# A kernel of attention and convolution on one core: edge rows wrapped in two steps, output weights prepared during attention

## The chip, the core and the metric

One core of a Trainium2 chip runs the kernel. The metric is the device time of one execution in microseconds. TensorE multiplies matrices, VectorE (DVE) and ScalarE (ACT) work on what it leaves in PSUM, GpSimd (POOL) works on SBUF, and SyncE (SP) issues nearly all transfers, in order, from one queue. The same 16 DMA engines carry all of them.

## The reference, cut to what matters

`_layer` is applied to a sample of 4096 rows (called s) and to a prompt of 1024 rows (p), both 1024 wide, in float32:

```python
proj = x @ w_in                                  # q, k, v, gate | three 512-wide inputs u_h | gate
attn = weights * three dilated windows of attention over q, k, v   # weights: softmax of their lse
u = _short_conv(u_h, conv_w, conv_b)             # out[t] = b + u[t-1] w0 + u[t] w1 + u[t+1] w2, zero beyond the ends
z = u[..., :C]
for n in range(2):
    z = u[..., (n + 1) * C:(n + 2) * C] * (_two_sided_fftconv(z, filters...) + hyena_d[n] * z)
mixed = concat(_rms(attn, attn_norm_g) * silu(g_attn), _rms(z, hyena_norm_g) * silu(g_hyena))
out = mixed @ w_out
y = layernorm(alpha * x + out)
```

## The kernel before

Products run in two rounded parts: an operand is split into a high part (`rnd`, usually ScalarE) and a remainder (`rest`, VectorE or POOL), and three products are summed.

Two chains of generators are woven together by `_interleave`, which gives each step a nominal length and always takes the chain that is behind; a step may yield the name of a flag and is held until that flag is in `self.done`. A planner then orders each engine's instructions by this order and by simulated readiness, so that what is emitted early has precedence. The first chain is `proj_first` (u0, u1, v; rows in groups of 128, first s, then p), `proj_second` (u2, k, q), `attention` (which begins with the gate), `last` and `output`. The second is `filters`, `convs`, `hyena`. Attention needs the PSUM that `convs` holds; `hyena` runs beside attention, its last eight row groups (those of p) after it, and `output` follows them.

A group r of 128 rows holds the positions a * R + r, so the neighbour of a row lies in the next or the previous group at the same a, and `short_conv` adds whole groups. Only group 0 and group R - 1 need a neighbour that is shifted by one a. Their parts go to a DRAM tile `e` (four parts of 128 rows), and a function `wrap` (lines 438 to 444) finishes them: it zeroes a tile on VectorE, loads 127 shifted rows of `e` into it, loads the other part, adds the two on POOL (line 417) and stores a row group of `u`, all at one place of the program. There are 12 wraps (three inputs, two sequences, two ends). Those of u0 and u1 of s run in the first group of p, those of p at the end of the first step of `proj_second`, those of u2 of s after its last group there, and those of u2 of p late in the gate of attention. `conv_in` reads u0 from group 0 on, after the flag `u_s`.

`conv_in`, `conv_mid` and `conv_out` are the convolution by two-stage Fourier transforms, with intermediate results in DRAM (X, B, G).

`output` loads w_out in 16 pieces of 128 x 512 by `load_w` (lines 382 to 395): load, scale by the norm weights `ng` (line 392), `rnd` to `wo h`, `rest` to `wo l` (line 227). Its loop multiplies the three attention results (`oo`, line 1271), normalizes, transposes and projects.

Of the kernel before, what the change touches and what calls it, by code (L numbers as in the profile page):

```python
# [10 lines left out]
F32 = mybir.dt.float32  # L11
# [186 lines left out]
class _Kernel:  # L198
# [31 lines left out]
    def scratch(self, ctx):  # L230
        dp = self.pool(ctx, "dram", 1, DRAM)
        self.S = {}
        for nm, L in SEQS:
            NB = L // N1
            self.S[nm] = dict(
                L=L, NB=NB, A=L // 16,
                x=self.I["x_" + nm],
                R=L // P,
                u=[dp.tile([L, C], F32, name=f"u{i}_" + nm) for i in range(3)],
                e=[dp.tile([4, P, C], F32, name=f"e{i}_" + nm) for i in range(3)],  # L240
                qT=dp.tile([C, L], F32, name="qT_" + nm),
                kT=dp.tile([C, L], F32, name="kT_" + nm),
                v=dp.tile([L, H, VW], BF16, name="v_" + nm),
                o=dp.tile([3, L, H, 66], F32, name="o_" + nm),
                G=[dp.tile([2 * N1, NB, C], F32, name=f"G{i}_" + nm) for i in range(2)],
                X=[dp.tile([2 * N1, NB, C], F32, name=f"X{i}_" + nm) for i in range(2)],
                B=[dp.tile([2 * NB, N1, C], F32, name=f"B{i}_" + nm) for i in range(2)],
                xT=dp.tile([D, L], F32, name="xT_" + nm),
                ga=dp.tile([L, C], F32, name="ga_" + nm),
                mx=dp.tile([L, C], F32, name="mx_" + nm),  # L250
            )

    def globals_(self, ctx):
        nc = self.nc
        gp = self.pool(ctx, "one")
        self.ident = gp.tile([P, P], F32, name="ident")
        with self.tc.high_priority():
            nc.sync.dma_start(out=self.ident, in_=self.I["ident"])
        self.one = gp.tile([P, 1], F32, name="one")
        nc.vector.memset(self.one, 1.0)  # L260

# [153 lines left out]
    def short_conv(self, tp, w, st, nm, i, r, ps, later):  # L415
# [3 lines left out]
        R, e = S["R"], S["e"][i]  # L419
# [18 lines left out]
        def wrap(tp, src, dst, part, row, tags=("m2", "m2")):  # L438
            z, y = (tp.tile([P, C], F32, name=tag) for tag in tags)
            nc.vector.memset(z, 0.0)  # L440
            nc.sync.dma_start(out=z[dst], in_=e[src][slice(1, P) if dst.start == 0 else slice(0, P - 1)])
            nc.sync.dma_start(out=y, in_=e[part])
            add(y, z)
            nc.sync.dma_start(out=ur[row], in_=y)

        later.append(lambda tp, **k: wrap(tp, 0, slice(0, P - 1), 3, R - 1, **k))
        later.append(lambda tp, **k: wrap(tp, 2, slice(1, P), 1, 0, **k))


    def proj_first(self, ctx):  # L450
# [49 lines left out]
        for b, (nm, r) in enumerate(work):  # L500
            S = self.S[nm]
            for ci in range(3):
# [22 lines left out]
                if r == 0 and later:  # L525
                    for f in later:
                        f(tp)
                    self.done.add("u_" + work[b - 1][0])
                    later.clear()
                yield 5.3  # L530
            cur, nxt = nxt, []
        self.later = later


    def proj_second(self, ctx):
# [37 lines left out]
        for b, (nm, g) in enumerate(work):  # L573
# [39 lines left out]
            if b == 0:  # L613
                for f in self.later:
                    f(tp)
                self.done.add("u_" + SEQS[-1][0])
            if last and b < len(work) - 1:
                for f in later:
                    f(tp)
                later.clear()  # L620
            self.later = later
# [9 lines left out]
    def convs(self, ctx):  # L631
# [3 lines left out]
        yield "u_" + a  # L635
        yield from self.conv_in(a)
        yield from self.conv_mid(a, 0)
        yield "u_" + b
# [5 lines left out]
        yield from self.conv_mid(b, 1)  # L644
        yield "qk"
# [19 lines left out]
    def conv_in(self, nm):  # L665
        nc, S = self.nc, self.S[nm]
        zr = S["u"][0].rearrange("(m n) c -> n m c", n=S["NB"])
        for n2 in range(0, S["NB"], 2):
            z = self.slot("z", ZB)
            for j in range(2):  # L670
                nc.sync.dma_start(out=z[64 * j:64 * j + 64], in_=zr[n2 + j])
            self.conv_dft(nm, 0, n2, z)
            yield 2.0

    def conv_mid(self, nm, n):
# [7 lines left out]
        for s in range(NB):  # L683
            x = self.slot("x", XB)
# [82 lines left out]
    def attention(self, ctx):  # L767
# [79 lines left out]
        with ExitStack() as gx:  # L847
            for i, v in enumerate(self.gate(gx)):
# [5 lines left out]
                if i >= 9 * BOOT and i % 10 == 0 and self.later:  # L854
                    self.later.pop(0)(lp, tags=("kT", "qT"))
# [288 lines left out]
    def hyena(self, ctx):  # L1144
# [4 lines left out]
        with self.tc.high_priority():  # L1149
            (wh, wl), = self.load_w(wp, self.stage(tp, "x", (NK, P), 2), self.I["w_in"][0], [7 * C], "wg")  # L1150
        yield "att"
        for nm, L in SEQS:
# [6 lines left out]
            for r in range(R):  # L1159
                x = tp.tile([P, NK, P], F32, name="x")  # L1160
# [46 lines left out]
    def output(self, ctx):  # L1207
# [6 lines left out]
        stp = [lambda: tp.tile([P, D], F32, name="hh", bufs=hbufs)[:, 0:512]]  # L1214
        ng = wp.tile([P, NK], F32, name="ng")
        nc.sync.dma_start(out=ng[:, 0:4], in_=self.I["attn_norm_g"][0].rearrange("(k p) -> p k", p=P))
        nc.sync.dma_start(out=ng[:, 4:8], in_=self.I["hyena_norm_g"][0].rearrange("(k p) -> p k", p=P))
        wt = {i: [wp.tile([P, NK, 512], F32R, name=f"wo{k}{i}") for k in "hl"] for i in range(2)}
# [13 lines left out]
        with self.tc.high_priority():  # L1232
            nxt = load(*work[0])
            wo = self.load_w(wp, stp, self.I["w_out"][0], [0, C], "wo", scale=ng, tiles=wt)
# [159 lines left out]
```

## Time and profile before

| | us |
|---|---|
| median of 3 runs | 4419.52 |
| lowest and highest | 4416.1, 4421.64 |
| the profiled execution | 4421.58 |
| its span in the profile | 4419.8 |

| engine | busy us of the span |
|---|---|
| TensorE (PE) | 4038.2 (91%) |
| VectorE (DVE) | 3218.0 (73%) |
| ScalarE (ACT) | 2152.8 (49%) |
| GpSimd (POOL) | 2003.6 (45%) |

How to read the rows: a row of the windows has the stretch in us from the start of the span, its length, the busy time and the number of instructions of PE, of its weight loads (PEld), of DVE, ACT and POOL, then the granted TensorE clock as a share of 2.4 GHz, the mean busy share of the 16 DMA engines and the GB/s that they moved. A row of the chain of waits has a start, a duration and what lasted so long; SPq is the queue that issues transfers, and a DMA row is a transfer from its issue to its landing. A row of the waits names who waited for whom, the total, the count and the longest. A row of the groups has line, engine, operation, output and input, shapes, count, then total and mean ns. A row of the timeline has a start, a duration, engine, line and operation.

### The profile page before, as it was taken

Reading aid. Unit: us, or ns where it says so; the run is one execution under the profiler, and the core shown is the slowest. Engines: PE = TensorE matmul, PEld = TensorE weight load, DVE = VectorE, ACT = ScalarE, POOL = GpSimd, SP = SyncE. Lnnn points to the kernel's source line nnn. Section 1 sums busy time; section 2 is a strip of 40 time slices with the busy share of each in tenths; the row PEclk is TensorE's granted clock in tenths of the full one; section 3 lists DMA queues with packets and bytes.
Section 4 is the critical chain, followed back from the end, with each engine's and each line's share of the span. In section 5 each row is a group of like instructions: output and inputs, shape, how many; then the busy total and the mean of one; then the engine's idle time right before and its main releaser. Section 6 shows DMA issues by size and latency. Waiting matters only on the chain.

```text
span 4419.8 us, 87947 instructions
## 1 busy us (share of the span) xinstructions
PE 4038.2 (91%) x31996; PEld 3416.6 (77%) x31996; DVE 3218.0 (73%) x6503; ACT 2152.8 (49%) x4246; POOL 2003.6 (45%) x1714
## 2 busy tenths in 40 slices
PE   7999999868789999998989979999999999689897
PEld 6999999858579876887867647888888887477776
DVE  7889888447678754575788666878787877677774
ACT  3433334245344444443465446777777776223332
POOL 4444444335567731366655251414141432266664
PEclk9999999979899999999989988999999999799999
DMA  5555555579555579754566665656565556644441
GB/s 182 180 179 171 178 171 176 178 223 284 166 162 165 165 253 285 230 160 142 170 211 195 215 205 152 175 154 170 155 180 153 153 159 176 217 169 173 173 173 67
DMA packets 662475, 800.87 MB, mean 181 GB/s; under 512 B 68024, under 2 KB 400014, under 8 KB 662042
## 3 DMA queue, kind: packets, MB, share of 16 engines
q1 hardware_dynamic: 643610, 762.64, 55.4%
q0 software_dynamic: 18432, 32.60, 3.2%
q8 instruction: 254, 4.16, 0.4%
q14 instruction: 179, 1.47, 0.1%
HBM read 499.22 MB, written 295.80 MB: 180 GB/s over the span
## 4 chain that ended last, share of the span: by engine, by line
PE 55%; DMA 13%; DVE 10%; POOL 7%; issue 6%; ACT 3%; SPq 2%; POOLq 0%; DVEq 0%; ACTq 0%
PE qk L401 10%; PE u L401 10%; PE pv L950 6%; PE sc L891 5%; PE pt L924 4%; PE g L1182 4%; PE g L1131 3%; POOL hh L1309 2%; DMA oo<-o_s 2%; POOL oo L1271 2%; PE pf L215 2%; PE g L215 2%; PE pz L215 2%; PE c L735 1%; PE c L215 1%
## 5 line engine op out<-in xcount | busy, mean ns | idle before, releaser
L223 POOL TENSOR_SCALAR qc<-q 128x256 fp32r<-128x256 f32 x352 | 246.9, 719 | 707.6 <-PE sc L891 702.0
L401 PE MATMUL u<-wuh,xh 128*128 128x256 f32 x1920 | 556.2, 290 | 10.0 <-ACT wuh L219 9.2
L401 PE MATMUL u<-wul,xh 128*128 128x256 f32 x1920 | 549.1, 286 | 2.2 <-DVE wul L227 2.0
L401 PE MATMUL u<-wuh,xl 128*128 128x256 f32 x1920 | 547.7, 285 | 2.1 <-DVE xl L227 2.1
L227 DVE TENSOR_TENSOR x<-x,xh 128x512 fp32r<-128x512 f32 x320 | 357.7, 1140 | 248.4 <-ACT xh L219 245.6
L915 ACT ACTIVATE sb<-sb,ob 128x192 f32<-128x192 f32 (+2 forms) x960 | 412.2, 473 | 39.9 <-DVE ob L906 31.3
L401 PEld LDWEIGHTS u<-wuh,xh 128*128 128x128 f32 x1920 | 371.6, 194 | 22.8 <-ACT wuh L219 10.4
L401 PEld LDWEIGHTS u<-wul,xh 128*128 128x128 f32 x1920 | 371.8, 194 | 11.9 <-DVE wul L227 3.0
L401 PEld LDWEIGHTS u<-wuh,xl 128*128 128x128 f32 x1920 | 371.4, 193 | 9.9 <-DVE xl L227 2.9
L401 PE MATMUL qk<-xh,wql 128*128 128x256 f32 x1280 | 364.2, 285 | 0.7 <-DVE wql L227 0.5
L401 PE MATMUL qk<-xh,wqh 128*128 128x256 f32 x1280 | 364.4, 285 | 0.0
L401 PE MATMUL qk<-x,wqh 128*128 128x256 f32 x1280 | 364.2, 285 | 0.0
L927 ACT ACTIVATE th<-pt 96x512 f16<-96x512 f32 (+2 forms) x480 | 272.1, 576 | 177.7 <-PE pt L924 174.8
L950 PE MATMUL pv<-V,th 128*128 128x64 bf16 (+3 forms) x5568 | 334.8, 194 | 0.0
L950 PE MATMUL pv<-V,tl 128*128 128x64 bf16 (+3 forms) x3712 | 324.5, 195 | 8.5 <-DVE tl L935 5.4
L935 DVE TENSOR_TENSOR tl<-pt,th 96x512 f16<-96x512 f32 (+2 forms) x480 | 316.2, 667 | 18.8 <-ACT th L927 16.6
L704 POOL TENSOR_TENSOR z<-fa,fi 128x512 f32<-128x512 f32 x160 | 246.2, 1539 | 151.2 <-DVE fi L703 150.5
L227 POOL TENSOR_TENSOR g<-g,gh 128x512 fp32r<-128x512 f32 x160 | 221.1, 1383 | 183.0 <-ACT gh L219 171.4
L219 ACT ACTIVATE xh<-x 128x512 fp32r<-128x512 f32 x400 | 241.9, 633 | 127.4 <-DMA x<-xT_s 42.2
L950 PEld LDWEIGHTS <-th 128*128 128x128 f16 (+1 forms) x5568 | 291.5, 98 | 2.2 <-issue 2.2
L950 PEld LDWEIGHTS <-tl 128*128 128x128 f16 (+1 forms) x3712 | 252.1, 98 | 51.1 <-DVE tl L935 17.6
L924 PE MATMUL pt<-ident,sb 128*128 128x128 f32 (+1 forms) x1856 | 291.1, 283 | 0.3 <-DVE tl L935 0.3
(223 smaller groups left out, 12021.5 us busy)
## 6 DMA issues: line engine op xcount, KB each, us to landing
G_s<-go SPq DMA_DIRECT2D x128, 256.0 KB
g<-G_s SPq DMA_DIRECT2D x128, 256.0 KB
x<-X_s SPq DMA_DIRECT2D x128, 256.0 KB
B_s<-bo SPq DMA_DIRECT2D x128, 256.0 KB
x<-xT_s SPq DMA_DIRECT2D x64, 512.0 KB
oo<-o_s SPq DMA_DIRECT2D x32, 792.0 KB
u_s<-m SPq DMA_DIRECT2D x96, 256.0 KB
V<-v_s SPq DMA_DIRECT2D x168, 145.5 KB
```

Source lines behind the costliest of these rows:

```text
L215: nc.tensor.matmul(out=out, lhsT=l, rhs=r, start=(i == 0), stop=(i == n - 1))
L219: self.nc.scalar.activation(out, in_, AF.Copy, scale=scale)
L223: self.nc.gpsimd.tensor_scalar(out=out, in0=in_, scalar1=scale, scalar2=0.0, op0=ALU.mult, op1=ALU.add)
L227: e.tensor_tensor(out=out, in0=in_, in1=hi.bitcast(F32), op=ALU.subtract)
L401: nc.tensor.matmul(out=out, lhsT=l, rhs=r, start=(k == 0 and i == 0), stop=(k == len(pairs) - 1 and i == len(ops) - 1))
L704: nc.gpsimd.tensor_tensor(out=z, in0=fa, in1=fi, op=ALU.add)
L891: nc.tensor.matmul(out=st["sc"][i], lhsT=qv[half, x], rhs=f(y)[half], start=(j == 0), stop=(j == 2))
L915: nc.scalar.activation(sb[:, i, 0:W], sb[:, i, 0:W], AF.Exp, bias=st["ob"][:, ui, i, 65:66], scale=-1.0)
L924: nc.tensor.transpose(out=pt[0:n, i, t], in_=st["pr"][:, i, t * n:(t + 1) * n], identity=self.ident)
L927: nc.scalar.activation(th[0:n, :, 0:nkt], pt[0:n, :, 0:nkt], AF.Copy)
L935: e.tensor_tensor(out=tl[0:n, :, 0:nkt], in0=pt[0:n, :, 0:nkt], in1=th[0:n, :, 0:nkt], op=ALU.subtract)
L950: last = nc.tensor.matmul(out=pv[:, 0:w], lhsT=st[p][0:n, i, t], rhs=vv[:, VC[b]:VC[b] + w], start=(t == 0 and j == 0), stop=(t == nkt - 1 ...
```

## The change

`e` gets a row of zeros at either end of its groups, stored once at the start, so that a shifted load reads 128 rows. `wrap` becomes two steps, `begin` (allocate and load) and `end` (add and store); `wrap_step` runs the `end` of the wraps begun before and begins one more. Steps are made in the row groups of p in `proj_first`, in `conv_mid`, and in the gate of attention. `conv_in` takes its row pairs from the middle on, each behind a flag of its row group, and the four that touch wrapped groups last, behind the flag `w_s` or `w_p`. `hyena` prepares the output's weights: in its row groups from the third on, one piece each, loaded, scaled, split and stored in a DRAM tile `wo`, in the buffer that its own input `x` uses. `output` only loads `wo`, in eight transfers of 1 MB.

```diff
--- before.py
+++ after.py
@@ -229,6 +229,7 @@
...
         dp = self.pool(ctx, "dram", 1, DRAM)
+        self.wo = dp.tile([2, NK, P, 2, 512], F32, name="wo")
         self.S = {}
@@ -237,7 +238,7 @@
...
                 u=[dp.tile([L, C], F32, name=f"u{i}_" + nm) for i in range(3)],
-                e=[dp.tile([4, P, C], F32, name=f"e{i}_" + nm) for i in range(3)],
+                e=[dp.tile([4, P + 2, C], F32, name=f"e{i}_" + nm) for i in range(3)],
                 qT=dp.tile([C, L], F32, name="qT_" + nm),
@@ -258,6 +259,13 @@
...
         nc.vector.memset(self.one, 1.0)
+        zero = gp.tile([P, C // P], F32, name="zero")
+        nc.vector.memset(zero, 0.0)
+        for nm, _ in SEQS:
+            for e in self.S[nm]["e"]:
+                for k, row in ((0, P + 1), (2, 0)):
+                    nc.sync.dma_start(out=e[k, row].rearrange("(p f) -> p f", p=P), in_=zero)
+        self.wraps, self.adds = [], []
@@ -416,7 +424,7 @@
...
         mul = lambda o, x: nc.vector.tensor_tensor(out=o, in0=ps, in1=x, op=ALU.mult)
-        R, e = S["R"], S["e"][i]
+        R, e = S["R"], [S["e"][i][k, 1:P + 1] for k in range(4)]
         ur = S["u"][i].rearrange("(a r) c -> r a c", r=R)
@@ -435,16 +443,27 @@
...
-        def wrap(tp, src, dst, part, row, tags=("m2", "m2")):
-            z, y = (tp.tile([P, C], F32, name=tag) for tag in tags)
-            nc.vector.memset(z, 0.0)
-            nc.sync.dma_start(out=z[dst], in_=e[src][slice(1, P) if dst.start == 0 else slice(0, P - 1)])
-            nc.sync.dma_start(out=y, in_=e[part])
-            add(y, z)
-            nc.sync.dma_start(out=ur[row], in_=y)
-
-        later.append(lambda tp, **k: wrap(tp, 0, slice(0, P - 1), 3, R - 1, **k))
-        later.append(lambda tp, **k: wrap(tp, 2, slice(1, P), 1, 0, **k))
+        def wrap(src, part, row):
+            def begin(tp, tags, **kw):
+                z, y = (tp.tile([P, C], F32, name=tag, **kw) for tag in tags)
+                nc.sync.dma_start(out=z, in_=src)
+                nc.sync.dma_start(out=y, in_=e[part])
+
+                def end():
+                    add(y, z)
+                    nc.sync.dma_start(out=ur[row], in_=y)
+                return end
+            return begin
+
+        later.append(wrap(S["e"][i][0, 2:P + 2], 3, R - 1))
+        later.append(wrap(S["e"][i][2, 0:P], 1, 0))
+
+    def wrap_step(self, *args, **kw):
+        for f in self.adds:
+            f()
+        self.adds = [f(*args, **kw) for f in self.wraps[:1]]
+        self.wraps = self.wraps[1:]
+        return not self.adds
@@ -522,14 +541,13 @@
...
                                   in_=vt.rearrange("p h c -> p (h c)"))
-                if r == 0 and later:
-                    for f in later:
-                        f(tp)
-                    self.done.add("u_" + work[b - 1][0])
-                    later.clear()
+                if nm != SEQS[0][0] and "w_" + SEQS[0][0] not in self.done and self.wrap_step(tp, ("wz", "wy"), bufs=1):
+                    self.done.add("w_" + SEQS[0][0])
+                if r == S["R"] - 1:
+                    self.wraps, later = later, []
+                self.done.add(f"u_{nm}{r}")
                 yield 5.3
             cur, nxt = nxt, []
-        self.later = later
@@ -610,15 +628,8 @@
...
                 yield 5.3
-            if b == 0:
-                for f in self.later:
-                    f(tp)
-                self.done.add("u_" + SEQS[-1][0])
-            if last and b < len(work) - 1:
-                for f in later:
-                    f(tp)
-                later.clear()
-            self.later = later
+            if last:
+                self.wraps, later = later, []
             cur, nxt = nxt, []
@@ -632,16 +643,17 @@
...
         a, b = (nm for nm, _ in SEQS)
-        yield "u_" + a
         yield from self.conv_in(a)
         yield from self.conv_mid(a, 0)
-        yield "u_" + b
         yield from self.conv_in(b)
...
         yield from self.conv_mid(b, 1)
+        for f in self.adds:
+            f()
+        self.adds = []
         yield "qk"
@@ -665,7 +677,12 @@
...
         zr = S["u"][0].rearrange("(m n) c -> n m c", n=S["NB"])
-        for n2 in range(0, S["NB"], 2):
+        R, NB = S["R"], S["NB"]
+        steps = [(f"u_{nm}{r + 2}", n2) for r in range(2, R - 2, 2) for n2 in (r, r + R)]
+        steps += [("w_" + nm, n2) for n2 in (R - 2, NB - 2, 0, R)]
+        for flag, n2 in steps:
+            if flag not in self.done:
+                yield flag
             z = self.slot("z", ZB)
@@ -681,6 +698,8 @@
...
         for s in range(NB):
+            if self.wrap_step(self.ct, ("fa", "fi"), bufs=2) and f"u_{SEQS[-1][0]}{self.S[SEQS[-1][0]]['R'] - 1}" in self.done:
+                self.done.add("w_" + SEQS[-1][0])
             x = self.slot("x", XB)
@@ -851,8 +870,8 @@
...
                     self.lead = None
-                if i >= 9 * BOOT and i % 10 == 0 and self.later:
-                    self.later.pop(0)(lp, tags=("kT", "qT"))
+                if i >= 9 * BOOT and i % 10 == 0:
+                    self.wrap_step(lp, ("kT", "qT"))
                 yield v
@@ -1148,6 +1167,21 @@
...
             (wh, wl), = self.load_w(wp, self.stage(tp, "x", (NK, P), 2), self.I["w_in"][0], [7 * C], "wg")
+        ng = wp.tile([P, NK], F32, name="ng")
+        nc.sync.dma_start(out=ng[:, 0:4], in_=self.I["attn_norm_g"][0].rearrange("(k p) -> p k", p=P))
+        nc.sync.dma_start(out=ng[:, 4:8], in_=self.I["hyena_norm_g"][0].rearrange("(k p) -> p k", p=P))
+        chunks = [(i, k) for i in range(2) for k in range(NK)]
+
+        def out_weights():
+            i, k = chunks.pop(0)
+            t = tp.tile([P, NK, P], F32, name="x").rearrange("p (a b) n -> p a (b n)", a=2)
+            lo, hi = t.bitcast(F32R)[:, 0], t.bitcast(F32R)[:, 1]
+            nc.sync.dma_start(out=t[:, 0], in_=self.I["w_out"][0, k * P:(k + 1) * P, i * 512:i * 512 + 512])
+            nc.vector.tensor_scalar_mul(t[:, 0], t[:, 0], ng[:, k:k + 1])
+            self.rnd(hi, t[:, 0])
+            self.rest(lo, t[:, 0], hi)
+            nc.sync.dma_start(out=self.wo[i, k], in_=t)
+
         yield "att"
@@ -1157,6 +1191,8 @@
...
             for r in range(R):
+                if chunks and r > 1:
+                    out_weights()
                 x = tp.tile([P, NK, P], F32, name="x")
@@ -1211,11 +1247,7 @@
...
         hbufs = 2 * G
-        stp = [lambda: tp.tile([P, D], F32, name="hh", bufs=hbufs)[:, 0:512]]
-        ng = wp.tile([P, NK], F32, name="ng")
-        nc.sync.dma_start(out=ng[:, 0:4], in_=self.I["attn_norm_g"][0].rearrange("(k p) -> p k", p=P))
-        nc.sync.dma_start(out=ng[:, 4:8], in_=self.I["hyena_norm_g"][0].rearrange("(k p) -> p k", p=P))
-        wt = {i: [wp.tile([P, NK, 512], F32R, name=f"wo{k}{i}") for k in "hl"] for i in range(2)}
+        wt = {i: [wp.tile([P, NK, 512], F32, name=f"wo{k}{i}") for k in "lh"] for i in range(2)}
         work = [(nm, n2) for nm, L in SEQS for n2 in range(0, L // P, G)]
@@ -1231,7 +1263,11 @@
...
             nxt = load(*work[0])
-            wo = self.load_w(wp, stp, self.I["w_out"][0], [0, C], "wo", scale=ng, tiles=wt)
+            for i in range(2):
+                for k in range(0, NK, 4):
+                    for t, w in enumerate(wt[i]):
+                        nc.sync.dma_start(out=w[:, k:k + 4], in_=self.wo[i, k:k + 4, :, t].rearrange("k p n -> p k n"))
+            wo = [[t.bitcast(F32R) for t in wt[i][::-1]] for i in range(2)]
         lng = wp.tile([P, D], F32, name="lng")
...
         nc.sync.dma_start(out=lng, in_=self.I["ln_g"][0:1].to_broadcast([P, D]))
```

## Rows read from the trace of the kernel before

**Rows 1.** Windows of the kernel before, stage by stage.

```profile
860.00:1085.00 225.00, 167.39 (x1191) 157.43 (x1190) 117.22 (x148) 95.46 (x169) 83.37 (x87) 0.86 0.74 229
870.00:920.00 50.00, 3.57 (x23) 2.65 (x21) 2.81 (x5) 2.47 (x4) 4.44 (x5) 0.55 0.24 74
920.00:930.00 10.00, 7.63 (x27) 6.25 (x28) 9.74 (x13) 6.24 (x11) 6.21 (x6) 0.51 0.81 261
930.00:1080.00 150.00, 141.74 (x1034) 134.62 (x1032) 98.08 (x121) 84.05 (x150) 69.36 (x74) 0.98 0.93 289
1170.00:1230.00 60.00, 25.00 (x103) 20.87 (x102) 19.52 (x28) 8.45 (x16) 21.12 (x16) 0.69 0.32 109
1990.00:2020.00 30.00, 12.63 (x54) 10.62 (x53) 8.73 (x12) 4.68 (x9) 11.87 (x10) 0.66 0.35 112
2510.00:2560.00 50.00, 34.54 (x119) 20.56 (x118) 16.06 (x24) 15.67 (x28) 4.88 (x7) 0.86 0.74 238
2580.00:2660.00 80.00, 54.61 (x159) 31.56 (x157) 59.92 (x80) 42.61 (x74) 61.41 (x48) 0.85 0.61 171
2800.00:3660.00 860.00, 840.03 (x12012) 707.58 (x12009) 678.04 (x2388) 629.37 (x1454) 274.18 (x349) 0.99 0.61 163
3740.00:3800.00 60.00, 39.12 (x150) 25.83 (x147) 41.49 (x97) 19.13 (x38) 20.41 (x16) 0.78 0.92 303
```

**Rows 2.** Chain of waits, the stretch of the first four wraps.

```profile
867.66 10.50 DMA m<-e_s
878.16 10.44 DMA u_s<-m
...
889.70 3.82 SPq L467
...
909.78 11.15 DMA z<-u_s
```

**Rows 3.** Chain of waits, the next six wraps.

```profile
1171.51 10.12 SPq L603
...
1192.83 13.41 DMA m<-e_p
...
1988.52 10.08 SPq L713
```

**Rows 4.** Waits of the whole span.

```profile
DVE m L440 <- DMA u_s<-m: 38.8, 2, 24.9
...
POOL m L417 <- DMA m<-e_s: 34.6, 3, 13.6
```

**Rows 5.** Groups of instructions of the whole span.

```profile
L417 POOL TENSOR_TENSOR m<-m,m 128x512 f32<-128x512 f32 x10 | 12.6, 1264 | 99.5 <-DMA m<-e_s 34.6 <-DMA m<-e_p 28.9 <-DVE m L440 24.8
...
L227 DVE TENSOR_TENSOR wol<-hh,woh 128x512 fp32r<-128x512 f32 x12 | 8.6, 713 | 1.6 <-ACT woh L219 1.6
...
L392 DVE TENSOR_SCALAR hh<-hh,ng 128x512 f32<-128x512 f32 x16 | 7.6, 488 | 0.7 <-DMA hh<-w_out 0.7
```

**Rows 6.** VectorE's timeline, the last eight rows of `hyena`.

```profile
3742.36 0.75 DVE L1201 SCALAR_TENSOR_TENSOR so<-zz,rsy,so 128x512 f32<-128x512 f32 x1
...
3760.07 1.00 DVE L1094 TENSOR_TENSOR rst<-rsy 128x1 f32<-128x1 f32 x1
...
3838.78 0.16 DVE L1094 TENSOR_TENSOR rst<-rsy 128x1 f32<-128x1 f32 x1
3839.36 0.75 DVE L1201 SCALAR_TENSOR_TENSOR so<-zz,rsy,so 128x512 f32<-128x512 f32 x1
...
3847.32 0.75 DVE L1201 SCALAR_TENSOR_TENSOR so<-zz,rsy,so 128x512 f32<-128x512 f32 x1
```

**Rows 7.** POOL's timeline, the same stretch.

```profile
3759.49 7.62 POOL L1271 TENSOR_TENSOR oo<-oo,ww 128x512 f32<-128x512 f32 x6
```

**Rows 8.** Chain of waits, the same stretch.

```profile
3749.43 7.45 DMA hh<-w_out
```

**Rows 9.** Timeline of the issuing queue, the start.

```profile
0.74 0.39 SPq L258 DMA_DIRECT2D ident<-ident  x1
```

## The prediction

> **What bounds the kernel now.** I read the windows first, stage by stage: TensorE is the bound. In attention it is busy 840.03 of 860 us, and around 930 to 1080 us, 141.74 of 150. Against that background a few holes stand out: 3.57 us of work in 870 to 920, 25.00 of 60 in 1170 to 1230, 12.63 of 30 in 1990 to 2020, and a shallower one, 34.54 of 50, in 2510 to 2560 [rows 1]. In the first three the DMA queues are nearly idle as well (share 0.24 to 0.35), so neither bandwidth nor arithmetic is short. The reader should ask who is waiting for whom.
>
> The chain of waits answers. In the first hole it runs through the wraps of `short_conv`: a load of `e` takes 10.50 us, the store of the wrapped row 10.44, and later `convs`' own load `z` lands after 11.15; between them the issuing queue itself stands for 3.82 us in front of a load of x [rows 2]. The other holes repeat it: the queue stands 10.12 us in front of a store of qT, POOL's operand `m<-e_p` takes 13.41, and a store of B is held 10.08 us [rows 3]. Behind the queue three engines stop: POOL's add waits for the load, VectorE's memset for the store of the wrap before (it needs that wrap's buffer), 24.9 us at the longest [rows 4]. VectorE and POOL execute in order, so the projection's own evictions stand behind them and TensorE runs out of free PSUM. There are 12 wraps, 4 in the first hole, 4 in the second, 2 in the third, 2 near 2500.
>
> **The change, part by part.** I make the sum against the profiled execution's own 4421.6 us, 2.1 above the median shown.
>
> *Wraps of s, first hole.* The add and the store of a wrap move to a later step, the zeroing goes, and the edge row now comes from a zeroed row in DRAM, so each load covers 128 rows instead of 127. Waiting vanishes from all three queues if the loads land within one step. At the busy share of the next stretch, 94.5%, the hole would hold 47.2 us of work and holds 3.6: 43.7 us. The next 10 us run at a granted clock of 0.51, the lower level (1.2 GHz) after that idling, so 7.63 us of work costs 3.7 too much: 47 in all. But the stretch 860 to 1085 moves 229 GB/s x 225 us = 51.5 MB; at the 289 GB/s sustained next door that needs 178 us, also 47 less; at 261 GB/s, the lowest of the loaded windows shown, 197, only 28 less [rows 1]. Bounds 28 and 47; I take 42, nearer the rate that 150 us sustain. The four adds remain, 1.26 us each on POOL [rows 5], which is busy under half of that stretch. `conv_in` must wait with its last four steps for the fifth row of the prompt. 28 of its 32 steps stand ahead of those and run beside the five rows, so I cost this at nothing; without that cover it costs one row, near 20 us (the 225 us less the hole, over eight rows of p), of the convolution chain alone.
>
> *Wraps of p, second hole.* They move into `conv_mid`, one per step. Idle is 35.0 us, and the 25.0 busy ran at a mean clock of 0.69, worth up to 8 more. If one transfer wait of about 10 stays, 25. I take 36, bounds 25 and 43.
>
> *Wraps of u2.* Third hole: idle 17.4, with its clock of 0.66 at most 21.7, with one 10 us wait left 7; I take 18. These two move into the last `conv_mid`, emitted after that point. There the convolution chain is alone on the path to attention (TensorE 54.61 of 80 us), so two more adds of 1.26 on POOL's queue and two buffers held for a step may cost 5. In the fourth hole 15.5 are idle, partly by other loads. Together I take a gain of 6, bounds +15 and -5.
>
> *Why 10 us.* The load that I blame carries 254 KB and takes 10.50 us while the DMA share of the whole hole is 0.24 [rows 1, 2]; few of the 16 engines can be at work. The Trainium skill, page "DMA: Bandwidth & Descriptors", section "Why a DMA increments its semaphore by 16 and not by 1", says that the number of engines divides the slowest dimension, 16 for 128 partitions and one for 127. By this rule the new loads are as quick as other loads of 256 KB; without it the 10 us would stay with the new shape, which is a rival below.
>
> *Output weights, the end.* Removed there: 16 scalings of 0.488 us, 16 roundings on ScalarE, 12 remainders of 0.713 on VectorE and 4 on POOL [rows 5]. They sit beside the last eight rows of `hyena`, which are a serial chain: from the last row of s to the last of p 104.96 us pass, and the last period alone is 7.96, so eight undisturbed rows need 64 and 41 are lost [rows 6]. Not all of it returns. While POOL multiplies `oo` (7.62 us, twice), VectorE's tiny rsqrt operations take 1.00 us instead of 0.16 [rows 6, 7]; ten slowed ones, 8 us, stay, and so do the loads of `oo` and `si`, for which I allow 5. And the weights now come as 8.39 MB instead of 4.19; at this stage's 303 GB/s the difference is 14 us in front of the rows' own loads. Taken: 41 - 8 - 5 - 14 = 14; bounds +41 and -14.
>
> *The same work inside attention.* 16 chunks, one per `hyena` row, each with a load, 1.2 us on VectorE (0.488 + 0.713), a rounding on ScalarE and a store of 512 KB. VectorE is busy 678 of 860 us there and TensorE already waits only 20 in 860 [rows 1]. If all of its VectorE time is exposed, 16 x 1.2 = 19 us; if it fills gaps, none. `hyena`'s `x` loses its second buffer in those rows but a row has some 30 us to load. I take a loss of 4, nearer to nothing because TensorE's waits there are 2% beside far more of the same VectorE work.
>
> *Start.* Twelve stores of zeros, at most 0.39 us of issue each [rows 9], 4.7 in all; they are not urgent, the weights beside them are. I take 1, bounds 0 and 5. Each has 128 runs of 16 bytes: the skill's same page ("Specifications") calls under 512 B below line rate, and no run here shows a price.
>
> Sum: 42 + 36 + 18 + 6 + 14 - 4 - 1 = 111. 4421.6 - 111 = 4310.6, and 2.1 less as a median: 4308.5.
>
> **Rivals.**
> *Transfers become the bound.* With the holes gone, the first stretch runs at 261 GB/s (28 instead of 42) and the end pays its 14 us with no gain (-14 instead of 14): 4308.5 + 14 + 28 = 4350. For it: share 0.93 and 0.92 in the two places. Against: 289 GB/s held for 150 us. 0.15.
> *The 10 us remain* whatever the number of rows, for instance because the rows were written just before. POOL and VectorE no longer wait, the queue still does, and half of the first three terms goes: 4356. Against: stores queued behind such loads are as late although their own shape is ordinary. 0.08.
> *The convolution chain, not TensorE, sets the start of attention* and gives the freed time back: it is alone in 2580 to 2660. Against: the held transfers z, g and B are its own. If half of the first two terms is lost, 4348; with the moved wraps in the way, 4360. 0.05.
> *Slower: VectorE waits for every chunk.* The planner places the scaling before the load has landed; such a load took 7.45 us [rows 8]. If each of 16 chunks stops VectorE so long and attention has no reserve: 16 x 7.45 = 119, in place of 4: 4424, and with the 19 us of work on top 4443. It decides from about 7.2 us a chunk. Against: the load is free to start a row earlier. 0.05.
> *More than forecast:* the end gains all 41 and the clock returns: 4264. 0.07.
>
> **How the numbers follow.** My forecast has 0.60, own range 4280 to 4335 from the middle of the bounds. All upper bounds give 4251, all lower 4400. The range 4264 to 4356 leaves out the slower case, most of the chain case and the edges. 0.2% is about what a measurement of this kernel can tell from no change (9 us): only the slower case, 0.05, lies above it, 0.02 for a cancellation, the rest faster.
>
> **What would show it.** Right: no `m<-e` wait near 10 us in the chain, no store standing 10 us on the issuing queue, TensorE above 85% after the first prompt row and at the start of the second projection, the last rows of `hyena` at 8 to 10 us each and about 14 us sooner relative to the end of attention, attention still above 96%. Wrong: 128-row loads of `e` at 10 us; a `w_out` load releasing VectorE inside attention; the convolutions' last stage longer than 85 us.

## The result, and the profile after

The changed kernel takes 4321.13 us (median of 4 runs, 4314.93 to 4324.31) against 4417.81 of before in the same session: ratio 0.9781, 95% interval 0.9764 to 0.9797. Forecast were 4308.5, with a range of 4264 to 4356. The profiled execution took 4324.31, its span is 4322.5, which is 97.3 less than the span of before.

The windows of the changed kernel, at the places of the holes of [rows 1] (columns as there):

```profile
860.00:1085.00 225.00, 208.16 (x1450) 193.07 (x1449) 175.00 (x204) 130.78 (x232) 126.16 (x118) 0.95 0.96 308
870.00:920.00 50.00, 50.00 (x390) 48.54 (x389) 36.39 (x44) 29.29 (x51) 26.54 (x28) 1.00 1.06 344
1170.00:1230.00 60.00, 58.09 (x355) 51.80 (x354) 50.98 (x62) 27.81 (x49) 43.62 (x32) 1.00 0.51 165
1990.00:2020.00 30.00, 28.74 (x176) 25.25 (x175) 21.81 (x29) 12.22 (x24) 23.45 (x16) 1.00 0.42 136
```

The three deep holes are gone: TensorE works 50.00 of 50 us where it worked 3.57, at the full clock, and the DMA engines move 344 GB/s where they moved 74. The waits for the edge rows that are left (who waited for whom, total, times, longest), where [rows 4] had 34.6 us and 13.6 at the longest:

```profile
POOL qT L425 <- DMA qT<-e_p: 6.9, 1, 6.9
POOL fi L425 <- DMA fi<-e_p: 4.3, 2, 3.1
POOL wy L425 <- DMA wy<-e_s: 2.5, 1, 2.5
```

A share of busy time doesn't say how far along the work is, so I measure progress by landmarks: the first and last start of one group of TensorE's products. Every stage has its own group: `g<-hhi,d` are the filters, `u` the first projection, `qk` the second, `sc<-kh,q` begins attention, `z` are the last eight rows of `hyena` (its first follows attention's end), `y` is the output. A row here has line, engine, operation, names, count, shortest, median and longest ns, then first and last start in us. Of before:

```profile
L215 PE MATMUL g<-hhi,d x320: 388/393/798, 80.9 to 844.9; 128*128 128x512 f32 x160
L401 PE MATMUL u<-wuh,xh x1920: 274/283/682, 24.2 to 1085.3; 128*128 128x256 f32 x192
L401 PE MATMUL qk<-xh,wqh x1280: 275/283/419, 1120.8 to 2202.8; 128*128 128x256 f32 x183
L1192 PE MATMUL z<-b,i x32: 592/643/1116, 3747.3 to 3836.3; 128*64 128x512 f32 x32
L215 PE MATMUL y<-woh,mh x640: 387/392/792, 3856.3 to 4399.6; 128*128 128x512 f32 x160
L891 PE MATMUL sc<-kh,q x512: 245/290/579, 2663.1 to 3377.8; 64*128 64x256 f32 x160, 64*128 64x192 f32 x11
```

The same groups after the change:

```profile
L215 PE MATMUL g<-hhi,d x320: 387/393/629, 94.4 to 856.0; 128*128 128x512 f32 x160
L409 PE MATMUL u<-wuh,xh x1920: 274/283/684, 24.2 to 1028.4; 128*128 128x256 f32 x192
L409 PE MATMUL qk<-xh,wqh x1280: 273/283/416, 1068.5 to 2083.5; 128*128 128x256 f32 x183
L1228 PE MATMUL z<-b,i x32: 592/1014/1117, 3641.0 to 3754.0; 128*64 128x512 f32 x32
L215 PE MATMUL y<-woh,mh x640: 387/392/632, 3694.9 to 4302.5; 128*128 128x512 f32 x160
L910 PE MATMUL sc<-kh,q x512: 246/291/580, 2546.3 to 3274.0; 64*128 64x256 f32 x160, 64*128 64x192 f32 x11
```

The differences of neighbouring landmarks, beside the terms of the prediction:

| stretch | before | after | gained | forecast (bounds) |
|---|---|---|---|---|
| start to last product of the filters | 844.9 | 856.0 | -11.1 | -1 (-5 to 0) |
| to last `u` (wraps of s) | 240.4 | 172.4 | 68.0 | 42 (28 to 47) |
| to last `qk` (wraps of p, two of u2) | 1117.5 | 1055.1 | 62.4 | 36 + 18 (32 to 65) |
| to first `sc` (the other two of u2, convolutions) | 460.3 | 462.8 | -2.5 | 6 (-5 to 15) |
| to first `z` (attention) | 1084.2 | 1094.7 | -10.5 | -4 (-19 to 0) |
| to last `y` (last rows, output) | 652.3 | 661.5 | -9.2 | 14 (-14 to 41) |
| sum | | | 97.1 | 111 |

So the total was met by terms that erred in opposite directions: the wraps brought more, the output's weights cost where a gain was forecast. The experiments had to settle three things: what in the wraps is worth so much, whether the weights really cost time, and where.

### The profile page after: what moved, and what is told of

It is laid out like the page before. It is cut to its first block, busy times and chain, and to the rows that moved or that the text cites. A ratio compares the mean times of both kernels' runs of the same rounds, so it can differ in the third digit from the quotient of the medians.

```text
span 4322.5 us, 87944 instructions
## 1 busy us (share of the span) xinstructions
PE 4019.1 (93%) x31996; PEld 3407.5 (79%) x31996; DVE 3214.5 (74%) x6496; ACT 2155.3 (50%) x4246; POOL 1996.0 (46%) x1710
## 5 line engine op out<-in xcount | busy, mean ns | idle before, releaser
L227 DVE TENSOR_TENSOR x<-x,xh 128x512 fp32r<-128x512 f32 x320 | 348.6, 1111 | 236.6 <-ACT xh L219 234.2
```

Source lines behind the costliest of these rows:

```text
L227: e.tensor_tensor(out=out, in0=in_, in1=hi.bitcast(F32), op=ALU.subtract)
```

## The experiments

All ratios are against the kernel before, run on the same chip in the same session. "Attention" is first `sc` to first `z`, "rows" first to last `z`, "end" first `z` to last `y`, each from the landmarks of that kernel's profile. (The expectations end attention 6 to 8 us before the first `z`, and so begin the end that much earlier.)

| kernel | us | ratio (95%) | first `sc` | attention | rows | end |
|---|---|---|---|---|---|---|
| before | 4417.8 | 1 | 2663.1 | 1084.2 | 89.0 | 652.3 |
| changed | 4321.1 | 0.9781 (0.9764 to 0.9797) | 2546.3 | 1094.7 | 113.0 | 661.5 |
| e1 wraps alone | 4301.6 | 0.9734 (0.9718 to 0.9751) | 2538.5 | 1084.9 | 87.9 | 655.4 |
| e2 weights alone | 4433.0 | 1.0031 (1.0019 to 1.0043) | 2660.6 | 1094.5 | 109.0 | 660.5 |
| e3 128 rows, one step | 4320.2 | 0.9778 (0.9763 to 0.9793) | 2561.8 | 1081.2 | 88.4 | 649.3 |
| e4 two steps, 127 rows | 4426.0 | 1.0018 (1.0008 to 1.0027) | 2648.2 | 1090.7 | 108.4 | 659.4 |
| e5 zero rows in 256 bytes | 4303.0 | 0.9743 (0.9727 to 0.9760) | 2540.1 | 1083.6 | 89.4 | 654.2 |
| e6 chunks later | 4317.7 | 0.9775 (0.9758 to 0.9792) | 2541.4 | 1092.2 | 109.5 | 662.2 |
| e7 weights behind rows | 4323.4 | 0.9787 (0.9771 to 0.9804) | 2544.3 | 1096.9 | 119.9 | 666.6 |
| e8 two steps, 112 and 16 rows | 4316.5 | 0.9776 (0.9758 to 0.9793) | 2539.1 | 1099.0 | 106.8 | 656.9 |
| e9 two pairs ahead | 4303.9 | 0.9745 (0.9731 to 0.9760) | 2528.7 | 1099.4 | 98.5 | 654.1 |
| e10 half the bytes | 4303.6 | 0.9747 (0.9730 to 0.9763) | 2541.2 | 1092.3 | 99.3 | 648.9 |
| e11 chunks, no arithmetic | 4304.7 | 0.9750 (0.9735 to 0.9764) | 2540.5 | 1085.4 | 114.7 | 665.2 |
| e12 chunks on POOL | 4306.4 | 0.9750 (0.9734 to 0.9767) | 2539.8 | 1089.9 | 99.1 | 653.2 |

### The two halves apart: e1 and e2

e1 is the changed kernel with the output's weights prepared at the end as before:

```diff
-                if chunks and r > 1:
-                    out_weights()
...
-            for i in range(2):
-                for k in range(0, NK, 4):
-                    for t, w in enumerate(wt[i]):
-                        nc.sync.dma_start(out=w[:, k:k + 4], in_=self.wo[i, k:k + 4, :, t].rearrange("k p n -> p k n"))
+            wo = self.load_w(wp, stp, self.I["w_out"][0], [0, C], "wo", scale=ng, tiles=wt)
```

> The two-step wraps and the zero rows alone; the output's weights are prepared at the end as in the kernel before. Theory of the prediction (the weights' part gains 14 at the end and costs 4 in attention): the wraps alone come 10 us above the changed kernel, near 4331. Rival, from laying the two traces' landmarks side by side (attention 10.5 us longer, its end to the end of the output 9.2 us longer): the weights' part costs about 20, so the wraps alone give about 4301. Both: attention (first score product to last value product) goes back from 1089 to 1078 us.

e2 is the other half, the same lines put into the kernel before:

> The output's weights prepared during attention, with the wraps of the kernel before. Theory of the prediction: 10 us faster than before, near 4408. Rival (landmarks): 20 us slower, near 4438, half of it between the first and the last product of attention and half behind it.

Both landed on the rival. The wraps alone give 4301.6, 19.5 below the changed kernel, and the intervals don't touch; the weights alone make the kernel before slower by 0.3% (14.8 us). With the 16 chunks (the pieces of weights) attention lasts 1094.7 (changed) and 1094.5 (e2), without them 1084.9 (e1) and 1084.2 (before); the end takes 661.5 and 660.5 with the prepared weights, 655.4 and 652.3 without. The forecast gain of 14 at the end doesn't exist. **e1 is faster than either kernel of the change, and no run has a lower median**, though the intervals of e5 and e9 to e12 overlap with its own.

### What makes the wraps worth 117 us: e3, e4 and e8

The change does two main things to a wrap: the load has 128 rows instead of 127, and the add comes a step later. With the second go the new places of the steps and the new order of `conv_in`. e3 does the first alone, all at one place of the program (in the kernel before, which gets the rows of zeros too):

```diff
-            nc.vector.memset(z, 0.0)
-            nc.sync.dma_start(out=z[dst], in_=e[src][slice(1, P) if dst.start == 0 else slice(0, P - 1)])
+            nc.sync.dma_start(out=z, in_=src)
```

> Kernel before with the rows of zeros and loads of 128 rows, but each wrap still done at one place of the program, all at the same places as before. Theory (the load of 127 rows itself is slow, 10.5 us, and holds the queue): the loads land in about 5 us, no store stands 10 us on the issuing queue, and half or more of the three holes goes: near 4365, between 4340 and 4385. Rival (waiting for any load and store at one place is the cost, whatever the rows): within 15 us of before, or slower by the 11 us that the start lost in the changed kernel.

e4 does the rest alone, in the changed kernel (`parts` are 127 rows and 1 row):

```diff
-                nc.sync.dma_start(out=z, in_=src)
+                for a, b in parts:
+                    nc.sync.dma_start(out=z[a:b], in_=src[a:b])
```

> The changed kernel with each shifted load split into one of 127 rows and one of the single row of zeros; nothing else differs. Theory (the 127 rows travel through one DMA engine and hold the queue): loads of 10 us return, the queue stands behind them, and a third to a half of the wraps' gain goes: 4350 to 4380. Rival (the second step covers the time of any load): 4321 to 4328.

e8 splits the same load into 112 and 16 rows: as many issues as e4, no load of 128 rows.

> The changed kernel with each shifted load split into 112 rows and 16 rows, one load more per wrap as in e4. Theory (the number of DMA engines that share a load is the largest that divides its rows, up to 16: 112 and 16 use all sixteen, 127 uses one): 4319 to 4327. Rival (anything that is not 128 rows, or the second load itself, is what cost e4 its 105 us): 4380 to 4430.

The shape of the load is nearly all of it, by more than my theory had it. With 128 rows and no second step, 98.0 us of the 116.7 of e1 are there; with two steps and 127 rows nothing is left: e4 at 4426.0 beside 4433.0 for e2, which has one step, 127 rows and the same weights. The second step, with the new places and the new order, is worth 18.7 us (e3 to e1) once the loads are quick; when they are not, the 7 between e2 and e4 are inside the spread of their runs (4425 to 4438 and 4416 to 4436). e3 and e4 both drop the zeroing on VectorE, which waited in [rows 4]; e4 shows that this brings nothing without the 128 rows. e8 removes the objection that e4 merely issues more loads: 4316.5, not slower than the changed kernel.

How a load that only one add needs can stop everything, e4 shows. Its chain of waits in the stretch of the first wraps (start, duration, what lasted so long; lines of under 6 us left out):

```profile
890.55 10.81 DMA wy<-e_s
901.38 6.19 DMA i<-i_s
...
908.61 15.56 DMA wz<-e_s
...
934.06 6.20 SPq L450
...
941.76 11.13 DMA z<-u_s
```

and the issuing queue's own waits between 850 and 1000 us:

```profile
SPq L689 <- DMA wz<-e_s: 8.0, 2, 6.4
SPq L707 <- DMA wz<-e_s: 6.1, 1, 6.1
SPq L451 <- DMA wz<-e_s: 6.1, 1, 6.1
```

A load of 127 rows, `wz`, takes 15.56 us. A load `wy` of 128 rows, issued behind the 127 rows of its own wrap, takes 10.81, and `z`, 64 rows for the convolutions, issued behind those of a later wrap, 11.13, where the median of such loads in the changed kernel is 4.4. Three places of the queue stand for `wz`, L689 and L707 with the convolutions' own loads. A later add cannot help, because what is late is not the add but everything that is issued after the load. In e3, where each add still stands directly behind its loads, POOL's waits for them are short (total, times, longest):

```profile
POOL m L423 <- DMA m<-e_s: 12.8, 4, 3.7
POOL m L423 <- DMA m<-e_p: 3.7, 4, 1.3
```

The Trainium skill, page "DMA: Bandwidth & Descriptors", section "Why a DMA increments its semaphore by 16 and not by 1", gives the number of engines of a transfer as the largest up to 16 that divides the slowest dimension of both its sides. By this rule 112 and 16 rows use sixteen engines and 127 rows use one; e8 and e4 agree with it, 4316.5 against 4426.0.

### The start: e5

The landmarks show 11 us lost before the filters' end. The issuing queue of the changed kernel there (start, duration, line, operation, count):

```profile
7.03 6.69 SPq L267 DMA_DIRECT2D e_s<-zero  x5
14.36 0.33 SPq L486 DMA_DIRECT2D xn<-x_s  x1
15.67 0.32 SPq L267 DMA_DIRECT2D e_p<-zero  x1
16.33 0.33 SPq L398 DMA_DIRECT2D t<-w_in  x1
```

Five stores of 2 KB take the queue 6.69 us, and the first weights are issued at 16.33. The kernel before issues them at 4.91:

```profile
4.91 0.76 SPq L390 DMA_DIRECT2D t<-w_in  x1
```

In e5 (based on e1) a row of zeros goes out in 8 runs of 256 bytes:

```diff
-                    nc.sync.dma_start(out=e[k, row].rearrange("(p f) -> p f", p=P), in_=zero)
+                    nc.sync.dma_start(out=e[k, row].rearrange("(p f) -> p f", p=8), in_=self.ident[64:72, 0:64])
```

> The wraps alone, as in e1, but each row of zeros is stored as 8 runs of 256 bytes (taken from zeros of the identity matrix) instead of 128 runs of 16 bytes; still 12 stores at the same place. Theory (the 12 us that the start lost are the price of 12 x 128 small pieces, in front of the first weights): the start returns to that of before, so 4290 against 4301.5 for e1. Rival (twelve more issues on the queue and their waits, whatever their size): 4298 to 4302.

The rival was nearer: 4303.0, where the theory had 4290. The size of the runs is not what holds the queue. Four stores of e5 still take it 5.25 us, and its waits between 3 and 17 us, in the changed kernel (L267) and in e5 (L264), are nearly the same, by the profile for the 512 KB loads of the convolution's taps issued just ahead:

```profile
7.18 5.25 SPq L264 DMA_DIRECT2D e_s<-ident  x4
...
SPq L267 <- DMA taps<-conv_w: 4.4, 3, 2.3
...
SPq L264 <- DMA taps<-conv_w: 4.0, 3, 2.0
```

The first weights go out at 13.71 in e5. Its first projection ends at 1023.0 instead of 1031.3 in e1 and the second at 2073.9 instead of 2082.0, but e9, with runs of 16 bytes, is there at 1025.7 and 2074.6, so these 8 us can't be put down to the runs either. Attention begins at 2540.1 instead of 2538.5, and the time is the same (4303.0 and 4301.6): the lead is gone by the end of the stretch between `qk` and `sc`, where gate and convolutions share the engines. What holds that end was not settled, and a kernel with the start of before was not run, so what the 11 us cost the total stays open.

### Attention: e6, e11 and e12

The eight kernels with the chunks' arithmetic on VectorE have attention at 1090.7 to 1099.4 (mean 1095.0), the four without the weights' part at 1081.2 to 1084.9 (mean 1083.5): 11.5 us for 16 chunks. e6 moves the chunks to later rows (`if chunks and r > 13`):

> The changed kernel with its 16 chunks in the row groups 14 to 29 of hyena instead of 2 to 17. Theory 1 (the 10 us that attention lost came in its first 70 us, when the clock is returning and VectorE and the queue are fullest; the later chunks cost nothing): attention lasts 1079 instead of 1087 us, total near 4313. Theory 2 (each chunk costs about 0.6 us of VectorE wherever it stands): attention stays at 1086 to 1088, total 4319 to 4323.

1092.2 with total 4317.7: between the two theories' totals, inside the eight's spread; the place matters little. e11 drops the arithmetic and keeps the transfers:

```diff
-            nc.vector.tensor_scalar_mul(t[:, 0], t[:, 0], ng[:, k:k + 1])
-            self.rnd(hi, t[:, 0])
-            self.rest(lo, t[:, 0], hi)
-            nc.sync.dma_start(out=self.wo[i, k], in_=t)
+            for j in range(2):
+                nc.sync.dma_start(out=self.wo[i, k, :, j], in_=t[:, 0])
```

> The changed kernel with the 16 chunks only loaded and stored (twice the same half, so as many bytes), without scaling, rounding and remainder; the output's weights are then wrong and the output is not the reference's. Theory 1 (the 10 us in attention are VectorE's and ScalarE's time for the arithmetic, 0.7 us a chunk, and VectorE's waits for the load): attention lasts 1075 to 1079 instead of 1087, total near 4311. Theory 2 (the chunk's 12.6 MB of transfers, the queue, and the buffer taken from hyena's x): attention stays at 1084 to 1089, total 4318 to 4323.

Attention 1085.4, within 2 us of the mean without chunks: the transfers are nearly free, the arithmetic is the price. With it the waits of VectorE for a chunk's load go as well; in the changed kernel, from the first chunk to the last, they are

```profile
DVE x L1180 <- DMA x<-w_out: 7.1, 7, 1.9
```

e12 takes e9 (below) and puts scaling and remainder on POOL, `nc.gpsimd.tensor_scalar_mul(...)` and `self.rest(lo, t[:, 0], hi, "pool")`:

> The kernel of e9 (prepared weights, two pairs ahead at the end) with the scaling and the remainder of the 16 chunks on POOL instead of VectorE; the rounding stays on ScalarE. Theory (VectorE's 1.2 us a chunk is what attention pays, POOL is busy for under a third of attention): attention comes back to 1076 to 1080 from 1087 to 1092, total 4290 to 4297, better than the wraps alone (4301.6). Rival 1 (ScalarE's rounding or the waits around a chunk are the price, whoever does the rest): attention 1084 to 1090, total 4301 to 4306. Rival 2 (POOL's work slows VectorE's small operations, as at the end): attention over 1090, total over 4306.

None of the three was met: attention is 1089.9 (about 1082 as the expectation counts it). That is 9.5 shorter than e9's and 5.1 below the mean of the eight, so about half of the price is back. The total (4306.4) is not told from e9's by its interval: the first `sc` comes 11.1 us later (2539.8 and 2528.7), before anything that this edit touches. On POOL the scaling takes 1.65 us instead of VectorE's 0.51.

The Trainium skill, page "Perfetto Trace Analysis", section "Optimizing Scalar/DVE Operations", warns that work moved between these two engines might not help, since they share a read port of SBUF. In attention it helped here, by 5 to 10 us; no run shows whether the port keeps the rest.

### The end: e7, e10 and e9

The rows take 113 us where the kernel before took 89, and the loop behind them is shorter (last `z` to last `y` 548.5 instead of 563.3). Waits of the changed kernel among the rows:

```profile
PE z L1228 <- DMA i<-i_p: 15.7, 1, 15.7
...
ACT xh L219 <- DMA x<-xT_p: 9.7, 1, 9.7
```

The rows' own loads `i` and `x` land late, behind 8.39 MB of weights. And POOL's multiplications of `oo` stand among the rows 30 times (five pairs) instead of 12 (two pairs). Its groups there, in the kernel before (columns as in [rows 5]):

```profile
L1271 POOL TENSOR_TENSOR oo<-oo,ww 128x512 f32<-128x512 f32 x12 | 14.7, 1260 | 0.0
```

and in the changed kernel:

```profile
L1307 POOL TENSOR_TENSOR oo<-oo,ww 128x512 f32<-128x512 f32 x30 | 34.1, 1170 | 77.7 <-DVE ww L1301 59.9 <-DVE rsy L1115 8.1 <-issue 7.0
```

e7 makes the weights' loads wait for the fourth of the eight rows (a value that this row writes goes into each weight tile first):

```diff
+                if nm == SEQS[-1][0] and r == 3:
+                    nc.vector.tensor_copy(out=self.mark, in_=so[:, 0:1])
...
+                        nc.vector.tensor_copy(out=w.bitcast(F32R)[:, k, 0:1], in_=self.mark)
                         nc.sync.dma_start(out=w[:, k:k + 4], in_=self.wo[i, k:k + 4, :, t].rearrange("k p n -> p k n"))
```

> The changed kernel, but the eight loads of the prepared weights (8.39 MB) wait for the fourth of the last eight rows of hyena instead of standing in front of all eight. Theory (the weights delay those rows' own loads, which sets the end): the eight rows take 89 us or less again instead of 113, the loop of the output starts 15 to 25 us sooner after the end of attention, total 4296 to 4308. Rival (the bytes must pass before the output starts, in whatever order): the same total within 5 us, 4316 to 4326.

The rival held: 4323.4. The rows got longer, not shorter (119.9): the seventh row now begins 32 us after the sixth (first products at 3721.3 and 3753.4). The chain of waits between the two runs through a load of weights and a store of the rows:

```profile
3722.93 14.26 DMA woh<-wo
3737.21 7.55 DMA mx_p<-so
```

So the bytes hold this row instead of the second and third. e10 loads half of them:

```diff
-                        nc.sync.dma_start(out=w[:, k:k + 4], in_=self.wo[i, k:k + 4, :, t].rearrange("k p n -> p k n"))
-            wo = [[t.bitcast(F32R) for t in wt[i][::-1]] for i in range(2)]
+                        if t:
+                            nc.sync.dma_start(out=w[:, k:k + 4], in_=self.wo[i, k:k + 4, :, t].rearrange("k p n -> p k n"))
+            wo = [[wt[i][1].bitcast(F32R)] * 2 for i in range(2)]
```

> The changed kernel with only the high parts of the prepared weights loaded (4.19 MB instead of 8.39); the products with the low part use the high part again, so the output is not the reference's. Theory 2 (bytes in front of the rows' loads): the eight rows lose 9 to 15 us of their 113 and the stretch behind attention goes from 669 to about 657, total near 4309. Theory 1 (VectorE and POOL hold the rows): the rows stay at 108 to 115, total 4317 to 4324.

e9 keeps the bytes and holds back the pairs from the third on, behind a value of the last row:

```diff
             mm = tp.tile([P, G, H], F32, name="mm")
+            if (nm, n2) not in work[:2]:
+                nc.vector.tensor_copy(out=mm[:, 0, 0:1], in_=self.mark)
```

> The changed kernel, but from the third pair of row groups on the output's mixing may not start on VectorE before the last row of hyena is done (before, two pairs stood among those rows; in the changed kernel five do). Theory 1 (the pairs that moved ahead hold VectorE and slow it, and that makes the eight rows 113 us instead of 89): the rows come back to 90 to 97 us and the stretch from the end of attention to the end of the kernel to 660 from 669; total near 4312. Theory 2 (the rows wait for their own loads behind the weights' 8.39 MB): the rows stay over 105 us and the total at 4319 to 4330, later rather than sooner.

Here my two theories were not rivals: each was right for a part, and no run combines the two edits. Landmarks of e10:

```profile
L1228 PE MATMUL z<-b,i x32: 592/850/1116, 3633.5 to 3732.8; 128*64 128x512 f32 x32
L215 PE MATMUL y<-woh,mh x1280: 387/392/776, 3673.4 to 4282.4; 128*128 128x512 f32 x183
```

and of e9:

```profile
L1229 PE MATMUL z<-b,i x32: 592/643/1116, 3628.1 to 3726.6; 128*64 128x512 f32 x32
L215 PE MATMUL y<-woh,mh x640: 387/394/628, 3683.2 to 4282.2; 128*128 128x512 f32 x160
```

With half of the bytes the rows take 99.3 and the end 648.9, 12.6 less than in the changed kernel; with two pairs ahead 98.5 and 654.1, 7.4 less (e12, with the same edit, has 99.1 and 653.2; the five kernels with the changed kernel's end have 656.9 to 662.2). Taking work forward into the rows saves nothing: with five pairs there instead of two the loop behind them is 7.1 us shorter (548.5 and 555.6) and the rows are 14.5 longer. The totals of both (4303.6, 4303.9) fell by more than the end explains; of e9's 17 us the profile has 7.4 at the end, and an attention that began 17.6 sooner and lasted 4.7 longer. The edit doesn't reach there, and that part stays open (last section).

## Why the prediction was right, and where it was wrong

**The diagnosis was right.** Loads of 127 rows hold the issuing queue; behind it POOL, VectorE and TensorE stop; the three holes went. The prediction named the row count as the cause and a rival in which 10 us stay with the new shape: no `e` load is waited for longer than 6.9 us, and e3, e4 and e8 show the row count by itself. What the prediction did not do is split the two halves of the change: it costed "The add and the store of a wrap move to a later step" and the zeroing beside the shape, and the shape, with the zeroing gone, is 98 of 117 us.

**First hole, 42 taken, 68 measured, bound 47 exceeded.** The failing step is the bound, in both ways in which it was taken. The windows between the two landmarks, before and after (columns as in [rows 1]):

```profile
844.90:1085.30 240.40, 182.79 (x1318) 172.76 (x1317) 126.10 (x157) 98.70 (x175) 90.31 (x95) 0.87 0.74 230
856.00:1028.40 172.40, 172.02 (x1313) 165.73 (x1312) 122.97 (x149) 96.64 (x169) 87.38 (x94) 1.00 1.00 316
```

TensorE does nearly the same number of products in both. Its idle time there was 57.6 us, of which 0.4 is left; the prediction took 43.7, from one window of 50 us and a busy share of 94.5%. The products themselves take 10.8 us less, at a granted clock of 1.00 instead of 0.87; the prediction took 3.7, from 10 us at the lower level. And the cap on the transfers, "51.5 MB; at the 289 GB/s sustained next door that needs 178 us", was none: 289 GB/s was what that neighbour asked for, and the changed kernel moves 316 between the landmarks and 344 from 870 to 920.

**Second and third hole, 54 taken, 62 measured**, inside the bounds.

**The moved wraps of u2, +6 taken, -2.5 measured**, inside the bounds; e1 has 3.8 there (from last `qk` at 2082.0 to first `sc`, 456.5 against 460.3). Kernels with the same order of instructions there take 454.1 (e9) to 462.8 (changed), so neither figure says much.

**Start, 1 taken with a bound of 5, 11 measured.** The step costed only the issue, 12 x 0.39. But the stores, and the queue's waits among them, stand ahead of the first weights, so these go out 11.4 us later (16.33 instead of 4.91), and in the first 250 us TensorE is busy for 208.96 us where it was for 218.80. What of this reaches the total is open (e5).

**Chunks in attention, 4 taken, 10.5 measured** (11.5 as a mean over twelve kernels), bounds 0 to 19. The reason given, that TensorE's 2% of waits leave cover for 19 us of VectorE work, was too kind: more than half of it is exposed. The rival "VectorE waits for every chunk" is there in small: 7 waits, 1.9 us at the longest instead of 16 of 7.45, since the loads do start early.

**The end, +14 taken, -9.2 measured.** This is the step that failed in sign: "eight undisturbed rows need 64 and 41 are lost", with the weights' arithmetic as the main cause of the 41. The 14 us for the doubled bytes were about right (e10 loads 4.19 MB less than the changed kernel, and its end is 12.6 shorter). But e10 has the bytes of before and none of the arithmetic, and its end is 648.9 against 652.3, hardly below the four kernels that keep the arithmetic there (649.3 to 655.4). So removing 16 scalings, 16 roundings and 16 remainders from the end, and taking three more pairs ahead, is together worth about 3 us. e9 prices the pairs at 7.4; if the two add, the arithmetic is worth some 11 us (an estimate), not the 28 taken (41 less 8 and 5). The rest of the 41 would then lie with the transfers and the output's own first pairs, which stayed; no run shows that split. The sign that the prediction set here, rows of 8 to 10 us each, was not met either: the eight take 113.0. The rival "transfers become the bound" had the end nearly right and the first stretch wrong.

**The total** came out within 13 us because +26 and +8 on the holes paid for -10, -8, -7 and -23 elsewhere, which is luck. The forecast was carried by the right mechanism with its weights misjudged in both halves.

## What to carry to other kernels

When a queue stands for some 10 us behind a transfer of ordinary size while the DMA engines idle, look at the number of rows of what was issued before it: one row of zeros that turned 127 rows into 128 was worth 98 us here, the rewriting of the steps 19. Before moving work out of a congested stretch, ask whether the arithmetic or the bytes congest it: storing prepared parts doubled the bytes where bytes were short, and put the arithmetic into attention, where it cost 11.5 us. And run the halves of a change apart: here a good and a bad one passed together for a success, and the good one alone is faster.

## What the runs showed that I had not expected

- A load of 127 rows delays its neighbours too: 64 rows of `z` took 11.13 us behind it, against a median of 4.4, and with such loads in place no gain of a later add is clear of the spread (7 us instead of 18.7).
- A dozen stores that nobody needs soon, issued ahead of the first weights, put these back by 11.4 us; in 4.4 of them the queue waited for other loads, and longer runs hardly changed that (five stores in 6.69 us, four in 5.25).
- The changed kernel, e7, e9 and e10 have the same order of instructions on every engine up to the last rows of attention, yet their profiles reach the first `sc` at 2546.3, 2544.3, 2528.7 and 2541.2 us. No run here tells what makes these 17.6 us (e7, e9 and e12 have one small tile more, and differ among themselves by up to 15.6: e12 is there at 2539.8). Terms of 10 us were therefore read from the stretch that an edit touches, not from totals.
